# Background loads on GpSimd's queue, queries and keys made in steps, and the output projection's operand built during the last pairs

## The chip, the cores and the metric

The kernel runs on one core of one Trainium2 chip. The metric is device time in microseconds (us) of one execution; the median of three runs of the kernel before is 2591.47 us (2590.05 to 2592.86). Engines are named as in the profile: PE is TensorE, PEld its weight load, DVE VectorE, ACT ScalarE, POOL GpSimd, SP SyncE, which here only issues DMAs.

## The reference, cut to what matters

One encoder layer over 1024 tokens of width 2048, in float32:

```python
h = rms_norm(x, pre_g)
proj = jnp.einsum('btd,dn->btn', h, w_in)          # 2048 -> 11264 columns
q, k, v, z_a, u, vs, z_b, g_a, g_b = jnp.split(proj, SPLIT_POINTS, axis=-1)
y_a = neighbourhood_attention(q, k, v, rpb, rows)   # 8 heads, 8 x 16 window, softmax with a bias
y_a = y_a * jax.nn.silu(z_a)
y_b = spatial_gating(u, vs, ln_g, ln_b, w_s, b_s) * jax.nn.silu(z_b)   # u * (W_s LN(vs) + b)
merged = (jax.nn.sigmoid(g_a) * jnp.einsum('btc,cd->btd', y_a, w_pa)
          + jax.nn.sigmoid(g_b) * jnp.einsum('btc,cd->btd', y_b, w_pb))
out = jnp.einsum('btd,de->bte', merged, w_out)
return x + rms_norm(out, post_g)
```

## The kernel before, in words

Each float32 operand is split in two float32r parts, a high one that ACT copies and a low one that DVE subtracts (`split`, L118); a product is three matmuls, high x high, high x low, low x high. `product` (L149) issues twelve matmuls of 128x512 for a weight block of 512 rows by 128 columns: one *step* of the sequence `seq` (L807).

The input projection and the two branch projections are cut in *pairs* of 2 x 128 output columns and 1024 input rows. A `Pair` (L159) computes its 2x2 blocks by Winograd's form of Strassen's scheme with seven products (p1, p2, p6, p5, p7, p4, p3) instead of eight: DVE forms the sums of weight blocks s1 to s4 (`prepare`), the sums t1 to t4 of the left operand are made once per operand (`Left`, L248), and `evacuate` brings the banks A, B and C back by ACT copies and DVE additions. A `PlainPair` (L215) takes eight products. The 2048 input rows make two halves f of 44 pairs each; the results of the first are stored in DRAM blocks `d_dram`, those of the second are added there by accumulating stores. All these stores are DMAs on POOL's queue (`store`, L288). Then come eight pairs for w_pb and eight for w_pa, whose results, times their gates, are stored and accumulated in `m_dram`; then the output projection with w_out.

The left operand (x for the halves, y_dram for the branches) lies split in eight slots of `apool`, named a0 to a7 with two tiles each. When the operand changes, `prepare_x` or `prepare_y` loads the next one into `ypool`, one yield per step, and `build` (L874) splits its parts into slots that the pair before no longer needs (`release`, L864). `build` runs `hook` as often as it takes until the sources have arrived.

The main loop (L911) does for each step: events due at this step, evacuation of the step before, a build, `hook()`, the weights' preparation for this step, the twelve matmuls, and preparation two steps ahead. `hook` advances the first generator of `tasks` by one yield; through it the rest of the layer runs beside the second half of the projections, in this order: `norms`, `values`, `layer_norms`, `gating` for 8 groups (4 yields each), `attention` for 8 heads, `first_gates` (sigmoids of the merge gates ahead of their use).

`attention` (L590) per head takes eight query tiles i in 11 yields: scores on PE into bank s; one DVE operation that adds the bias tile `bt` and finds the maximum `mx` (L651); the exponential and the scaling on ACT; transposes; products with `vk` three yields later; the gate `za`. The loads stand in SP's queue, in program order with the weights' loads (L141): raw queries and keys `qk` (`block`, L463), `vk` (L623), `za` (L629), bias (L636). `queries` and `keys` scale and split a head's `qk` tiles in one yield each. DMAs of one queue are issued in order, and a DMA whose buffer or source isn't ready holds those behind it.

In `gating` (L531), z is multiplied by r_rows (the tokens' 1/rms), passed through Silu, and multiplied by r_rows again; u is multiplied by it, and the result yb (one buffer) by u.

After the last step all pools are closed; tiles of the merged operand are loaded from `m_dram` on ACT's queue and split one by one (`load_merged`, `split_merged`, L999 to L1006) ahead of the step that uses them, w_out comes in chunks of 256 KB (`load_chunk`, L955). `wide_step` (L985) issues the twelve matmuls of one chunk for four token tiles.

## Time and profile before

| | |
|---|---|
| median of three runs | 2591.47 us |
| the profiled execution | 2593.09 us |
| its span | 2591.3 us |
| mean granted clock | 0.987 |
| PE, DVE, ACT, POOL busy | 97%, 55%, 41%, 14% |
| moved by DMA | 410.10 MB, mean 158 GB/s |

Matmuls are pipelined, so a busy PE is not a PE at its peak: how many matmuls are issued in a stretch tells more than its busy share. An idle time stands before the instruction that ended it, with what released it. The granted clock of a stretch is 1.00 at full speed and 0.50 at half.

### The profile page before, as it was taken

The numbers are of one execution on the slowest core, as the hardware profiler recorded it, in microseconds if no ns is written. First come the engines' busy times: TensorE is split into PE (matmuls) and PEld (weight loads), VectorE is DVE, ScalarE is ACT, GpSimd is POOL, SyncE is SP. The second block draws the span as 40 slices with busy tenths as digits, with TensorE's granted clock in tenths as the row PEclk, the third lists the DMA queues.
The fourth block names the chain that finished last, engine by engine and source line by source line (L and its number), as shares of the span: only waits on it lengthen the run. The fifth ranks groups of instructions, "written<-read, shape, count | busy, mean of one in ns | idle before, by whom it ended". The sixth has DMA issues, their size and how long they took to land.

```text
span 2591.3 us, 32620 instructions
## 1 busy us (share of the span) xinstructions
PE 2507.8 (97%) x11363; PEld 2074.0 (80%) x11363; DVE 1423.2 (55%) x2270; ACT 1058.0 (41%) x1883; POOL 358.6 (14%) x532
## 2 busy tenths in 40 slices
PE   7999999999999999999999888999999999899998
PEld 5888888888888788887787777788888888788887
DVE  6444444444444744577655544466676787542434
ACT  6533333333333534432365555544443434342332
POOL 1111111111111112122111111133311111000000
PEclk9999999999999999999999999999999999999999
DMA  5633333333334468777765566589975676753645
GB/s 174 209 126 110 117 106 115 106 110 118 106 114 171 98 130 212 159 176 179 172 175 144 134 158 157 142 240 279 235 195 161 223 170 152 184 162 98 203 121 192
DMA packets 240069, 410.10 MB, mean 158 GB/s; under 512 B 25736, under 2 KB 85152, under 8 KB 239264
## 3 DMA queue, kind: packets, MB, share of 16 engines
q1 hardware_dynamic: 178432, 253.30, 32.4%
q0 software_dynamic: 55968, 141.07, 23.4%
q10 hardware_dynamic: 5504, 13.65, 1.6%
q8 instruction: 89, 1.46, 0.2%
q14 instruction: 76, 0.62, 0.1%
HBM read 264.78 MB, written 143.13 MB: 157 GB/s over the span
## 4 chain that ended last, share of the span: by engine, by line
PE 54%; issue 32%; POOL 7%; ACT 2%; DMA 2%; DVE 1%; SPq 0%; POOLq 0%; ACTq 0%; DVEq 0%
PE A L153 23%; PE C L153 11%; PE B L153 6%; PE t L989 3%; PE A L989 3%; POOL m L293 2%; PE s L989 2%; PE B L989 2%; PE C L989 2%; PE v L989 2%; DMA bt<-bias 1%; POOL d_ga L293 1%; POOL g_gb L767 1%; POOL d_qk L293 1%; POOL d_zu L293 1%
## 5 line engine op out<-in xcount | busy, mean ns | idle before, releaser
L153 PE MATMUL A<-a,wh 128*128 128x512 f32 x3328 | 1037.8, 393 | 15.3 <-ACT wh L120 11.7
L153 PEld LDWEIGHTS A<-a,wh 128*128 128x128 f32 x3328 | 623.3, 189 | 143.4 <-ACT wh L120 13.0
L121 DVE TENSOR_TENSOR wl<-x,wh 128x512 fp32r<-128x512 f32 x616 | 423.3, 688 | 498.3 <-ACT wh L120 495.3
L153 PE MATMUL A<-a,wl 128*128 128x512 f32 x1664 | 652.2, 392 | 7.3 <-DVE wl L121 7.0
L153 PE MATMUL C<-a,wh 128*128 128x512 f32 x1664 | 521.2, 395 | 7.0 <-ACT wh L120 4.5
L120 ACT CAST wh<-x 128x512 fp32r<-128x512 f32 x616 | 380.9, 619 | 280.5 <-PE C L153 220.9
L202 ACT COPY u<-A 128x512 f32<-128x512 f32 x300 | 176.3, 588 | 524.5 <-PE A L153 522.1
L153 PEld LDWEIGHTS A<-a,wl 128*128 128x128 f32 x1664 | 314.3, 189 | 77.2 <-DVE wl L121 10.7
L153 PEld LDWEIGHTS C<-a,wh 128*128 128x128 f32 x1664 | 313.7, 190 | 72.5 <-ACT wh L120 5.8
L153 PE MATMUL C<-a,wl 128*128 128x512 f32 x832 | 327.7, 394 | 1.7 <-DVE wl L121 1.6
L197 DVE TENSOR_TENSOR u<-C,u 128x512 f32<-128x512 f32 x200 | 138.0, 690 | 244.8 <-ACT u L202 154.5
L153 PE MATMUL B<-a,wh 128*128 128x512 f32 x864 | 269.9, 393 | 1.8 <-ACT a L410 0.9
L153 PEld LDWEIGHTS B<-a,wh 128*128 128x128 f32 x864 | 162.4, 189 | 35.9 <-ACT a L410 1.3
L153 PEld LDWEIGHTS C<-a,wl 128*128 128x128 f32 x832 | 158.1, 190 | 36.9 <-DVE wl L121 3.4
L121 DVE TENSOR_TENSOR wl<-wr,wh 128x512 fp32r<-128x512 f32 x120 | 82.8, 691 | 188.8 <-ACT wh L120 188.8
L153 PE MATMUL B<-a,wl 128*128 128x512 f32 x432 | 170.2, 394 | 2.0 <-DVE wl L121 1.8
L120 ACT CAST wh<-wr 128x512 fp32r<-128x512 f32 x120 | 74.6, 623 | 215.7 <-PE t L989 187.4
L174 DVE TENSOR_TENSOR x<-x,x 128x512 f32<-128x512 f32 x200 | 137.7, 688 | 3.5
L120 ACT CAST wh<-s 128x512 fp32r<-128x512 f32 x100 | 62.0, 620 | 102.4 <-PE B L153 100.3
L989 PE MATMUL A<-wh,x 128*128 128x512 f32 x240 | 94.1, 392 | 5.6 <-ACT wh L120 3.2
L153 PEld LDWEIGHTS B<-a,wl 128*128 128x128 f32 x432 | 81.8, 189 | 21.2 <-DVE wl L121 4.2
L292 ACT COPY c<-A 128x512 f32<-128x512 f32 x88 | 51.7, 587 | 111.1 <-PE A L153 111.1
(181 smaller groups left out, 2605.9 us busy)
## 6 DMA issues: line engine op xcount, KB each, us to landing
x<-w_units SPq DMA_DIRECT2D x288, 256.0 KB
wr<-w_out SPq DMA_DIRECT2D x120, 256.0 KB
d_zu<-u POOLq DMA_DIRECT2D x48, 256.0 KB, 3.9
d_qk<-u POOLq DMA_DIRECT2D x48, 256.0 KB, 3.9
d_gb<-u POOLq DMA_DIRECT2D x48, 256.0 KB, 3.6
d_ga<-u POOLq DMA_DIRECT2D x48, 256.0 KB, 4.1
m<-u POOLq DMA_DIRECT2D x48, 256.0 KB, 4.2
x<-w_v SPq DMA_DIRECT2D x32, 256.0 KB
```

The lines of the kernel that those rows point to most:

```text
L120: nc.scalar.copy(out=hi, in_=src)
L121: nc.vector.tensor_tensor(out=lo, in0=src, in1=hi.bitcast(F32), op=ALU.subtract)
L153: nc.tensor.matmul(acc, lhsT=wt[:, j * P:(j + 1) * P], rhs=operand[j // 2][:, j % 2, part], start=(first and j == 0 and n == 0), stop=(j = ...
L174: nc.vector.tensor_tensor(out=out, in0=in0, in1=in1, op=op)
L197: nc.vector.tensor_tensor(out=out, in0=in0, in1=out, op=ALU.add)
L202: nc.scalar.copy(out=u, in_=acc["A"])
L292: nc.scalar.copy(out=t, in_=bank)
L293: nc.gpsimd.dma_start(out=dst[c], in_=t, **({"accum_op": ALU.add} if accumulate else {}))
L767: nc.gpsimd.dma_start(out=g_dram[pr][c], in_=t)
L989: nc.tensor.matmul(acc[i], lhsT=stat[:, part, t * P:(t + 1) * P], rhs=wt, start=(kt == 0 and part == 0 and wt is chunk[0]), stop=(kt == nk ...
```

## The change

Five parts. (1) `block`, `fetch_values` and `fetch_gate` issue their loads on POOL's queue (`nc.gpsimd`) instead of SP's. Bias tiles have four buffers instead of three and are requested three tiles ahead instead of two. (2) A head's queries and keys are made in four steps (`prelude`: scale the queries, split them, scale the keys, split them), at yields 7 to 10 of the head before; the yield between two heads is gone. (3) In `gating`, Silu stands a yield behind the multiplication of z, u is multiplied by r_rows in place of the second multiplication of z, and yb has two buffers. (4) At the start x comes by SP's queue alone and the first two weight blocks by ACT's, and the sums of the first left operand take the scale by g with them (`scaled_less`), in another order. The pool for the second half's operand is opened three pairs ahead instead of two. (5) `merges` is a task: it loads merged tiles on POOL's queue, the first two into a pool of their own, the others into slots of `apool` as the last pair's products let go of them; the first four chunks of w_out are loaded six steps before the projections end, into the weights' buffers; `hook()` is called in the output projection too. The pools are placed anew for it.

```diff
-    for w, name in zip(NAMES, ("x11", "x21", "x12", "x22")):
+    first.load(("x11", "x21"), nc.scalar)
+    for w, names in zip(NAMES, ((), (), ("x12",), ("x22",))):
         for j in range(4):
-            load_x(first_x[j // 2][w][:, j % 2], 0, w, j, nc.gpsimd if j % 2 else nc.sync)
-        first.load((name,))
+            load_x(first_x[j // 2][w][:, j % 2], 0, w, j, nc.sync)
+        first.load(names)
...
+        def scaled_less(jj, w, other, dst):
+
+            s = left.src[jj]
+            for j in range(2):
+                kt = x_tile(0, w, 2 * jj + j)
+                nc.vector.scalar_tensor_tensor(out=s[dst][:, j], in0=s[w][:, j], scalar=g_cols[:, kt:kt + 1],
+                                               in1=s[other][:, j], op0=ALU.mult, op1=ALU.subtract)
...
+        for step in (((t1, 0),), ((t1, 1), (t2, 0)), ((t2, 1), ("t2", 0)), (("t2", 1), (t3, 0)), ((t3, 1), ("t1", 0)),
+                     (("t1", 1), (t4, 0)), (("t3", 0), (t4, 1)), (("t3", 1),), (("t4", 0),), (("t4", 1),)):
...
     def block(pool, pr, n, hf, tag, bufs):
 
         t = pool.tile([P, HALF], F32, tag, bufs=bufs)
-        nc.sync.dma_start(out=t, in_=d_dram[pr][2 * n + hf])
+        nc.gpsimd.dma_start(out=t, in_=d_dram[pr][2 * n + hf])
         return t
...
+        yield
+        for hf in range(2):
             nc.scalar.activation(z[hf], z[hf], AF.Silu)
-        yield
         if ("zu", g + 1) in complete:
             fetch_group(g + 1)
         for hf in range(2):
-            nc.vector.tensor_tensor(out=z[hf], in0=z[hf], in1=r_rows[:, hf * HALF:(hf + 1) * HALF], op=ALU.mult)
+            nc.vector.tensor_tensor(out=u[hf], in0=u[hf], in1=r_rows[:, hf * HALF:(hf + 1) * HALF], op=ALU.mult)
...
-            yb = bpool.tile([P, HALF], F32, "yb")
+            yb = bpool.tile([P, HALF], F32, "yb", bufs=2)
...
+        def prelude(h):
+
+            return [lambda: scaled(h, 0), lambda: queries(h), lambda: scaled(h, 1), lambda: keys(h)]
...
-                nc.sync.dma_start(out=vk[:4 * w, b], in_=v_dram[h, :, COL0[b]:COL0[b] + w])
+                nc.gpsimd.dma_start(out=vk[:4 * w, b], in_=v_dram[h, :, COL0[b]:COL0[b] + w])
...
-                nc.sync.dma_start(out=zs[:, hf * HALF:(hf + 1) * HALF], in_=d_dram[("za", h // 2)][2 * (h % 2) + hf])
+                nc.gpsimd.dma_start(out=zs[:, hf * HALF:(hf + 1) * HALF], in_=d_dram[("za", h // 2)][2 * (h % 2) + hf])
...
-            bts[(h, i)] = pool.tile([P, KROWS * 32], F32, "bt", bufs=3)
+            bts[(h, i)] = pool.tile([P, KROWS * 32], F32, "bt", bufs=4)
...
-                    if i < 6:
-                        fetch_bias(h, i + 2)
+                    if i < 5:
+                        fetch_bias(h, i + 3)
                     scores(h, i)
...
-                if i == 5 and ("head", h + 1) in complete:
+                if i == 3 and ("head", h + 1) in complete:
                     fetch(h + 1)
...
+                    following = prelude(h + 1)
+                if following and i >= 7:
+                    following[i - 7]()
+                    if i >= 8:
+                        fetch_bias(h + 1, i - 8)
+                yield
             nc.gpsimd.dma_start(out=y_dram[h], in_=zs)
             del kept[h]
-            yield
...
-        at(where[(n - 2, "p1")], open_ypool, prepare)
+        at(where[(n - (3 if n == K2 else 2), "p1")], open_ypool, prepare)
...
+    def merges():
+
+        nonlocal mpool0, mpool
+        mpool0 = Pool(tc, "mpool0")
+        mpool = Pool(tc, "mpool")
+        raw = {}
+        for d in range(NDT + 1):
+            if d < NDT:
+                while ("m", d // 2) not in complete:
+                    yield
+                raw[d] = mpool.tile([P, T], F32, "mr", bufs=2)
+                for hf in range(2):
+                    nc.gpsimd.dma_start(out=raw[d][:, hf * HALF:(hf + 1) * HALF], in_=m_dram[d // 2][2 * (d % 2) + hf])
+            yield
+            if d:
+                d -= 1
+                while d >= 2 and (d - 2) // 2 >= len(free):
+                    yield
+                places[d] = (mpool0, f"m{d}") if d < 2 else (apool, f"a{free[(d - 2) // 2]}_{d % 2}")
+                merged[d] = x8(d)
+                split(merged[d][:, 0], merged[d][:, 1], raw.pop(d))
+            yield
...
+        if k == len(seq) - 6:
+            loaded.extend(load_chunk(n) for n in range(LOADS))
+        if k == len(seq) - 1:
+            advance(0)
...
             for kt in range(NDT - (LATE if last else 0)):
-                if tg == 0 and ep == 0 and kt + 2 < NDT:
-                    split_merged(kt + 2)
-                    if kt + 4 < NDT:
-                        load_merged(kt + 4)
+                while kt not in merged or kt == NDT - 1 and mpool:
+                    hook()
                 for e in range(2):
                     wide_step([a[e] for a in acc], merged[kt], kt, tiles, next_chunk())
                     step_active()
+                    hook()
```

How this moves instructions, at three places. First SP's queue, from the second bias load of one head (the fourth) on, before; bt is a bias tile, vk, za and qk are the head's other loads, x the weights' blocks of the projections:

```order
L636 DMA bt<-bias 128x384
L623 DMA vk<-v_dram 96x1x512
L623 DMA vk<-v_dram 128x1x512 x2
L623 DMA vk<-v_dram 96x1x512
L636 DMA bt<-bias 128x384
L636 DMA bt<-bias 128x288
L141 DMA x_11947<-w_units 128x512
L141 DMA x_11949<-w_units 128x512
L636 DMA bt<-bias 128x288
L629 DMA za<-d_za_2_186 128x512
L629 DMA za<-d_za_3_187 128x512
L636 DMA bt<-bias 128x384
```

and a head's stretch of the same queue now:

```order
L672 DMA bt<-bias 128x384
L672 DMA bt<-bias 128x288
L141 DMA x_12063<-w_units 128x512
L141 DMA x_12146<-w_units 128x512
L672 DMA bt<-bias 128x288
L672 DMA bt<-bias 128x384
L141 DMA x_12258<-w_units 128x512
L141 DMA x_12260<-w_units 128x512
L672 DMA bt<-bias 128x384
L672 DMA bt<-bias 128x288
```

Bias and weights are left in SP's queue; the four vk, two za and four qk loads of a head are gone from it.

Second, POOL's queue in attention, from one head's store of y_dram on, before; d_qk and d_za are result blocks of the projections, stored from the tiles u and c:

```order
L731 DMA y_dram_69<-za 128x1024
L293 DMA d_qk_3_167<-u_11462 128x512
L293 DMA d_qk_2_166<-c_11539 128x512
L293 DMA d_za_0_188<-u_11499 128x512
L293 DMA d_qk_1_165<-u_11402 128x512
L293 DMA d_za_3_191<-u_11759 128x512
```

and now:

```order
L762 DMA y_dram_69<-za 128x1024
L659 DMA vk<-v_dram 96x1x512
L659 DMA vk<-v_dram 128x1x512 x2
L659 DMA vk<-v_dram 96x1x512
L293 DMA d_qk_3_167<-u_11458 128x512
L665 DMA za<-d_za_0_184 128x512
L665 DMA za<-d_za_1_185 128x512
L293 DMA d_qk_2_166<-c_11535 128x512
L492 DMA qk<-d_qk_0_160 128x512
L492 DMA qk<-d_qk_1_161 128x512
L492 DMA qk<-d_qk_2_162 128x512
L492 DMA qk<-d_qk_3_163 128x512
```

The stores keep their order, and ten loads of a head now stand between them, za behind the y_dram store that reads the same buffer.

Third, DVE in gating, from the last multiplication of one group to the first steps of the next, before; wl is the low part of a weight block, bs the bias of the spatial gating:

```order
L563 TENSOR_TENSOR yb<-yb,u 128x512
L121 TENSOR_TENSOR wl<-s_9436,wh 128x512
L197 TENSOR_TENSOR u_9403<-C,u_9403 128x512
L542 SCALAR_TENSOR_TENSOR bs<-t,lnb,bs 128x128
L545 TENSOR_TENSOR z<-z,r_rows 128x512 x2
L121 TENSOR_TENSOR wl<-x_9215,wh 128x512
L551 TENSOR_TENSOR z<-z,r_rows 128x512 x2
L121 TENSOR_TENSOR wl<-x_9428,wh 128x512
```

and now:

```order
L590 TENSOR_TENSOR yb<-yb,u 128x512
L121 TENSOR_TENSOR wl<-s_9430,wh 128x512
L197 TENSOR_TENSOR u_9397<-C,u_9397 128x512
L568 SCALAR_TENSOR_TENSOR bs<-t,lnb,bs 128x128
L571 TENSOR_TENSOR z<-z,r_rows 128x512 x2
L121 TENSOR_TENSOR wl<-x_9209,wh 128x512
L578 TENSOR_TENSOR u<-u,r_rows 128x512 x2
L121 TENSOR_TENSOR wl<-x_9422,wh 128x512
```

The place of the second multiplication of z is taken by that of u, whose load stands in POOL's queue behind the y_dram store of the group before.

## Rows read from the trace of the kernel before

**Rows 1.** The page's first part: engine, busy us, share, instructions.

```profile
PE 2507.8 (97%) x11363; PEld 2074.0 (80%) x11363; DVE 1423.2 (55%) x2270; ACT 1058.0 (41%) x1883; POOL 358.6 (14%) x532
```

**Rows 2.** The chain of waits, 150 to 200: start, us, what.

```profile
162.38 2.72 PE B L153 x12
```

**Rows 3.** Windows by stage: length, busy time (instructions) by engine, clock, DMA share, GB/s.

```profile
10.65:56.47 45.82, 38.99 (x144) 29.92 (x145) 36.76 (x46) 32.65 (x52) 2.71 (x5) 0.93 0.48 145
847.66:857.43 9.77, 7.55 (x25) 5.50 (x24) 5.71 (x7) 7.88 (x13) 1.08 (x2) 0.83 0.19 58
1125.99:1248.57 122.58, 114.94 (x553) 94.60 (x552) 93.36 (x153) 41.01 (x72) 24.63 (x34) 0.97 0.75 186
1281.31:1694.18 412.87, 373.51 (x1910) 314.59 (x1909) 215.41 (x470) 228.55 (x463) 50.81 (x62) 0.95 0.60 151
2209.26:2245.69 36.43, 29.47 (x110) 22.29 (x108) 17.17 (x23) 12.45 (x18) 3.49 (x5) 0.91 0.73 182
```

**Rows 4.** Windows of clean steps, one group of gating and parts of heads.

```profile
1128.86:1141.79 12.93, 12.93 (x69) 11.02 (x68) 9.41 (x16) 4.96 (x9) 2.29 (x3) 1.00 0.72 189
1485.76:1495.86 10.10, 10.10 (x49) 8.59 (x50) 7.40 (x17) 5.18 (x12) 3.15 (x4) 1.00 0.82 184
1295.38:1299.52 4.14, 4.14 (x25) 3.65 (x25) 2.62 (x6) 2.23 (x6) 0.00 (x0) 1.00 0.96 324
1346.72:1374.42 27.70, 27.70 (x158) 24.22 (x157) 15.90 (x37) 19.69 (x41) 2.55 (x3) 1.00 0.57 144
```

**Rows 5.** Waits of PE in attention: who for whom, us, times, longest.

```profile
PE s L647 <- DVE mx L651: 30.4, 7, 9.0
```

**Rows 6.** Waits of all engines in attention.

```profile
DVE pr L651 <- DMA bt<-bias: 51.6, 7, 12.2
```

**Rows 7.** Window of the last two microseconds of one stop.

```profile
1448.00:1450.00 2.00, 0.00 (x0) 0.00 (x0) 0.00 (x0) 0.00 (x0) 0.00 (x0) 0.50 0.54 194
```

**Rows 8.** Timeline of SP's queue before that stop: start, us, what.

```profile
1430.97 4.05 SPq L623 DMA_DIRECT2D vk<-v_dram  x4
1435.37 5.13 SPq L636 DMA_DIRECT2D bt<-bias  x2
```

**Rows 9.** Timeline of DVE at its end; in brackets the idle time before.

```profile
1450.45 0.56 DVE L651 CUSTOM_DVE_ANT_0 pr<-s,bt 128x384 f32<-128x384 f32 x1 [10.18 <-DMA bt<-bias]
```

**Rows 10.** The tile y_dram, 1100 to 1700: its stores (ns, min/median/max) and their landing.

```profile
L564 POOL DMA_DIRECT2D y_dram<-yb x16: 561/572/577, 1138.0 to 1253.1; - x16
...
DMA to landing us min/median/max: 2.3/4.2/8.7
```

**Rows 11.** Waits of all engines in gating.

```profile
DVE yb L560 <- DMA y_dram<-yb: 19.0, 8, 3.2
```

**Rows 12.** Timeline of DVE in gating, between two groups.

```profile
1171.93 0.69 DVE L563 TENSOR_TENSOR yb<-yb,u 128x512 f32<-128x512 f32 x1
...
1176.49 0.69 DVE L121 TENSOR_TENSOR wl<-x,wh 128x512 fp32r<-128x512 f32 x1 [1.21 <-ACT wh L120]
1177.10 1.29 DVE L551 TENSOR_TENSOR z<-z,r_rows 128x512 f32<-128x512 f32 x2
```

**Rows 13.** Timeline of POOL at the same place.

```profile
1174.12 0.85 POOL L293 DMA_DIRECT2D d_zu<-u  x1 [0.63 <-DVE bs L542]
```

**Rows 14.** The tile y, 0 to 60: landing of POOL's loads.

```profile
DMA to landing us min/median/max: 6.6/8.0/9.0
```

**Rows 15.** Timeline of ACT at the start.

```profile
4.25 0.72 ACT L410 ACTIVATE a<-y,g_cols 128x512 fp32r<-128x512 f32 x1 [1.57 <-DMA g_cols<-pre_g]
8.14 1.95 ACT L410 ACTIVATE a<-y,g_cols 128x512 fp32r<-128x512 f32 x3 [3.17 <-DMA y<-x_t]
9.99 0.60 ACT L120 CAST wh<-x 128x512 fp32r<-128x512 f32 x1
```

**Rows 16.** Groups of instructions: busy us, mean ns, idle before.

```profile
L121 DVE TENSOR_TENSOR x<-mr,x 128x1024 fp32r<-128x1024 f32 x16 | 19.6, 1226 | 9.5 <-ACT x L120 9.5
```

**Rows 17.** Window of the last steps of the projections.

```profile
2200.00:2210.00 10.00, 10.00 (x46) 8.29 (x45) 8.14 (x13) 3.81 (x8) 2.58 (x3) 1.00 0.63 137
```

More of the change, by code (lines that the diff above doesn't have):

```diff
@@ L687, in attention @@
         for h in range(H):
-            while h not in raw and h not in kept:
-                if ("head", h) in complete:
-                    fetch(h)
+            if h not in kept:
+                while ("head", h) not in complete:
                     yield
-                yield
-            if h not in kept:
-                queries(h)
-                yield
-            if len(kept[h]) < 2:
-                keys(h)
-                yield
-            if (h, 0) not in bts:
-                fetch_bias(h, 0)
-            fetch_bias(h, 1)
+                fetch(h)
+                for i in range(3):
+                    fetch_bias(h, i)
+                    yield
+                for f in prelude(h):
+                    f()
+                    yield
             fetch_values(h)
-            yield
+            following = None
             for i in range(11):
@@ L890, in build @@
             ypool.close()
+            if left is left_of[3]:
+                begin(merges)
     def need(left, part):
@@ L894, in need, with x8 @@
             build()
+    LATE = 4
+    LOADS, AHEAD = 4, 2
+    jobs, loaded, ready = [], [], []
+    taken = [0]
+    active = []
+    for tg in range(2):
+        for ep in range(2):
+            jobs += [w_out[kt, 2 * ep + e] for kt in range(NDT) for e in range(2)]
+    del jobs[-2 * LATE:]
+    mpool0 = mpool = None
+    merged, places = {}, {}
+    def x8(d):
+        pool, tag = places[d]
+        return pool.tile([P, 2, 2, HALF], F32R, tag).rearrange("p a b t -> p a (b t)")
+    def merges():
[8 more added lines that the diff above has]
+                raw[d] = mpool.tile([P, T], F32, "mr", bufs=2)
+                for hf in range(2):
+                    nc.gpsimd.dma_start(out=raw[d][:, hf * HALF:(hf + 1) * HALF], in_=m_dram[d // 2][2 * (d % 2) + hf])
[3 more added lines that the diff above has]
+                while d >= 2 and (d - 2) // 2 >= len(free):
+                    yield
+                places[d] = (mpool0, f"m{d}") if d < 2 else (apool, f"a{free[(d - 2) // 2]}_{d % 2}")
+                merged[d] = x8(d)
+                split(merged[d][:, 0], merged[d][:, 1], raw.pop(d))
+            yield
+        mpool.close()
+        mpool = None
@@ new lines, in load_chunk, with advance @@
+    def load_chunk(n):
+        raw = wpool.tile([P, HALF], F32, ("x11", "x12")[n % 2], bufs=2)
+        nc.sync.dma_start(out=raw, in_=jobs[n])
+        return raw
+    def advance(now):
+        while len(loaded) < min(now + LOADS, len(jobs)):
+            loaded.append(load_chunk(len(loaded)))
+            if len(ready) < len(loaded) - (LOADS - AHEAD):
+                ready.append(split_weights(loaded[len(ready)]))
+        while len(ready) < min(now + AHEAD, len(jobs)):
+            ready.append(split_weights(loaded[len(ready)]))
@@ new lines, in next_chunk, with step_active, wide_step @@
+    def next_chunk():
+        advance(taken[0] + 1)
+        pair = ready[taken[0]]
+        taken[0] += 1
+        return pair
+    def step_active():
+        for g in list(active):
+            if next(g, StopIteration) is StopIteration:
+                active.remove(g)
+    def wide_step(acc, stat, kt, tiles, chunk, nk=NDT):
+        for i, t in enumerate(tiles):
+            for part, wt in ((0, chunk[0]), (0, chunk[1]), (1, chunk[0])):
+                nc.tensor.matmul(acc[i], lhsT=stat[:, part, t * P:(t + 1) * P], rhs=wt,
+                                 start=(kt == 0 and part == 0 and wt is chunk[0]),
+                                 stop=(kt == nk - 1 and part == 1))
@@ L896, in hybrid_kernel, with wide_banks @@
+    def wide_banks(tiles):
+        return [[psum(a), psum(b)] for _, (a, b) in zip(tiles, (("A", "A"), ("B", "C"), ("s", "v"), ("t", "t")))]
     starting = first_builds()
@@ L980, in step_active @@
-    def step_active():
-        for g in list(active):
-            if next(g, StopIteration) is StopIteration:
-                active.remove(g)
-    def wide_step(acc, stat, kt, tiles, chunk, nk=NDT):
-        for i, t in enumerate(tiles):
-            for part, wt in ((0, chunk[0]), (0, chunk[1]), (1, chunk[0])):
-                nc.tensor.matmul(acc[i], lhsT=stat[:, part, t * P:(t + 1) * P], rhs=wt,
-                                 start=(kt == 0 and part == 0 and wt is chunk[0]),
-                                 stop=(kt == nk - 1 and part == 1))
@@ L993, in wide_banks @@
-    def wide_banks(tiles):
-        return [[psum(a), psum(b)] for _, (a, b) in zip(tiles, (("A", "A"), ("B", "C"), ("s", "v"), ("t", "t")))]
-    merged, raw_m = {}, {}
-    def load_merged(d):
-        raw_m[d] = p4.tile([P, T], F32, "mr", bufs=2)
-        for hf in range(2):
-            nc.scalar.dma_start(out=raw_m[d][:, hf * HALF:(hf + 1) * HALF], in_=m_dram[d // 2][2 * (d % 2) + hf])
-    def split_merged(d):
-        merged[d] = x8(d if d < 15 else 16)
-        split(merged[d][:, 0], merged[d][:, 1], raw_m.pop(d))
```

172 lines of the change are left out of this document (73 added, 99 removed).

## The prediction

> **What bounds the kernel.** I first read the busy shares [rows 1]: PE is busy 97% of the span, DVE 55%, ACT 41%, POOL 14%. That points at PE, but does not say how well it is fed, so the second view is the chain of waits in a clean stretch [rows 2]: twelve matmuls of 128x512, one step of the sequence, take 2.72 us. The program has 860 such steps (100 Pairs of 7 and 4 PlainPairs of 8 in the projections, 128 in the output projection), 2339 us of a span of 2591.3. The rest is small matmuls, which stay, and losses. For the losses I read busy time and clock by stage [rows 3] against clean steps [rows 4].
>
> - Start: the first matmul is at 10.65, and the 12 steps after it take 45.82 instead of 32.64: 13.2 lost.
> - Change of operand before the second half: two steps in 9.77, 4.3 lost.
> - Gating: 34 steps in 122.58. A clean group of four steps takes 12.93, 2.05 more than 4 x 2.72; 34 x 2.72 + 8 x 2.05 = 108.9, so 13.7 is lost.
> - Attention: 412.87 for 8 heads of 11 steps and 7 steps between heads. The clean pieces [rows 4] make one head: 10.10 (its first three steps) + 4.14 (the fourth) + 27.70 (the last seven) = 41.94. 8 x 41.94 + 7 x 2.72 = 354.6, so 58.3 is lost.
> - Way into the output projection: 9 steps in 36.43 instead of 24.48, 12.0 lost.
>
> That is 101.5, beside the 10.65 ahead of the first matmul. Over half is in attention. There PE stands still 412.87 - 373.51 = 39.4 us [rows 3], 30.4 of it in seven waits of the scores for DVE's mx [rows 5], and DVE is late because a bias tile is: 51.6 in seven waits [rows 6]. The other 18.9 of the 58.3 is mostly the half clock (1.2 instead of 2.4 GHz) behind a stop: the granted mean is 0.95 in this stage [rows 3] and was 0.50 late in one stop [rows 7]. So a microsecond of PE's wait costs 1.5 here. Why the bias is late stands in SP's queue [rows 8]: four vk loads are issued ahead of it, the issue of two bias loads then takes 5.13, and DVE waits 10.18 until the tile has landed [rows 9].
>
> **The change, part by part.**
>
> *Attention, loads.* vk, za and qk (10 DMAs a head) leave SP's queue for POOL's; bias goes from two steps ahead with 3 buffers to three with 4. SP then holds weights and bias alone. The mechanism that I take: bias waited for what stood ahead of it in one queue, not for the engines, since late in the stop, with PE, DVE, ACT and POOL all idle, the DMA share was only 0.54 [rows 7]. With one step more of lead (10.10 / 3 = 3.4 us) and four loads fewer ahead, all seven waits go: 30.4 x 1.5 = 45.6. *Attention, compute.* Scaling and splitting of queries and keys become four steps instead of two, so ACT's casts no longer stand behind a DVE operation of the same step. Of the 12.7 that is left of the loss I let 5 stay: 53 gained. Bounds: 58.3, and 0 if bias lands as late as now.
>
> The Trainium skill says in DMA: Bandwidth & Descriptors, section Issuing engines are not separate DMA queues, that the DMAs of all issuing engines run on the same 16 engines, and that issuing from several saves issue time alone; by it the move of vk is worth little, and the time would be that of rival A. The same page, section Queues, rings and completion order, has each engine take turns between queues, which would let bias pass vk. The 0.54 agrees better with the second; no run here has vk on another queue.
>
> *What POOL takes on.* Per head 10 issues of 0.57 (a plain issue, [rows 10]), 5.7 us in 42, on an engine that is 14% busy. The stores of u and c wait behind them. The za load waits for the landing of the y_dram store of the head before (one za buffer), up to 8.7 [rows 10]; it stands two steps behind that store now, four before. The u1 buffer is used again seven steps later, some 26 us in this stage, so I cost these waits at nothing; rivals B and C are the cases in which that cover is gone.
>
> *Gating.* Two of DVE's waits go: yb for its own store, 19.0 in eight [rows 11], by a second buffer, and a wl in each group, 1.21 [rows 12], whose cast stands behind the Silu that waits for z: 9.7 in eight. One comes: u is multiplied by r_rows a step before it was needed, and its loads go to POOL behind the y_dram store. From the end of the last yb multiply (1172.62) to the place where u stands now (1177.10) DVE has 4.5 less 1.2 of wait, 3.3 us of work [rows 12], and 3.9 to the second half. POOL needs 0.57 for the store, 0.57 for the first load, and in half of the groups 0.85 for a u store between [rows 13]. No row has a plain load on POOL here; the nearest are the y_dram stores, most of them of 256 KB, median 4.2 to landing [rows 10], and the loads at the start, median 8.0 with eight queued at once [rows 14]. I take 5, nearer to the stores, since POOL's queue is short here: 0.57 + 0.57 + 0.43 + 5 - 3.9 = 2.7 a group, 21.6 against the 28.7 removed. At 13.7 lost for 28.7 of DVE's waits 10.3 stays: 3.4 gained. Bounds: 13.7 gained (2.3 to landing, no wait), 8 lost (8.0 to landing, 5.7 a group).
>
> *Operand before the second half.* prepare_x needs 4 + 16 yields, one a step, but its pool opens 14 steps ahead, and build() then runs what is left at once, with ACT busy 7.88 of the 9.77 [rows 3]. It opens 21 steps ahead now: 4 of 4.3 gained, 0 if ACT is late for another reason.
>
> *Start.* x comes by SP alone, the first two weight blocks by ACT's queue, and 12 of 16 scalings on ACT become part of DVE's subtractions. Now ACT waits 3.17 for a tile by POOL's queue [rows 15], which took 6.6 or more to land [rows 14], while SP's first tile was there by 4.25. Four scalings 0.65 apart and the cast end at 4.25 + 2.6 + 0.6, say 7.7: 3 gained. Of the 13.2 behind it the wait for the weight block goes, and ACT's work shrinks by 12 x 0.65 = 7.8; DVE's stays. I take 7. Bounds for both: 0 and 16.
>
> *Output projection.* The merged tiles are loaded and split during the last steps and placed where the last pair's operands were; four weight chunks are loaded ahead. PE's idle time there, 36.43 - 29.47 = 7.0 [rows 3], and the half clock behind it go, 12.0 at most. But four splits of 1.23 [rows 16] now stand in DVE's last eight steps, and DVE was busy 8.14 of 10 there [rows 17]: 17.7 + 4.9 = 22.6 in 21.8. No slack is left, so I keep 3.5: 8.5 gained, and 0 if DVE falls behind.
>
> Sum: 53 + 3.4 + 4 + 10 + 8.5 = 78.9. The profiled execution took 2593.09 (the span of 2591.3 and 1.8 around it), which gives 2514.2; the median shown is 1.6 lower, so **2512.6**, with a range of its own from 2495 to 2526.
>
> **Rivals.**
>
> *A: the engines, not the queue, make bias late* (or the weight loads ahead of it, which wait for buffers, so that the move doesn't do what it says). For it: a DMA share of 0.60 over the stage and 0.73 to 0.75 in two others [rows 3]. Against: 0.54 in the stop. Then only the lead helps: 3.4 off each of seven waits of 4.3 on average and 9.0 at most [rows 5] leaves 7 to 13, say 10, x 1.5 = 15: 2527.
>
> *B: loads on POOL are slow, 8 to 9 us as at the start.* Gating loses 8 instead of gaining 3.4. And za is late for the fifth step of each head: 8.7 for the y_dram store and 8.5 for the load against 14.2 from the head's start (10.10 + 4.14) is 3 late, 8 x 3 x 1.5 = 36, and half of it if DVE's lead takes the rest. 2512.6 + 11.4 + 18 = 2542. For it: POOL serves one queue in order. Against: the stores on it land in 4.2.
>
> *C, slower: POOL's queue stands still.* A load that waits for a landing (qk for d_qk's accumulating store, za for y_dram's) holds the u stores behind it; ACT's next copy into u1 waits, every cast behind it too, and PE stops with the clock halved. It decides where POOL stands for longer than the 26 us of u1 less 9 for issue and landing, 17 us. To use up the gain it takes 78.9 / 8 = 9.9 a head, 6.6 of stop x 1.5; at 11 a head the time is 2512.6 + 88 = 2601. Against it: the longest landing of these on POOL is 9.0 [rows 14].
>
> *D: gains and new waits are equal*: 2586 to 2597.
>
> **Chances.** Forecast 0.64, A 0.15, B 0.13, C 0.06, D 0.02. The range from 2495 to 2548 holds the forecast, A and most of B; left out are C, D, a worse B, and a gain above 97. A measurement of this kernel tells a change of over 0.2%, 5.2 us, from none: faster 0.92, same 0.02, slower 0.06.
>
> **What would show it.** No wait of DVE for bt over 1 us, and heads of 42 to 43 us, show the main step; waits for bt in the same place, shorter by 3 to 4, show A. DVE's waits for u<-d_zu in gating tell what a load on POOL takes; waits for za or vk show B, ACT's waits for the landing of u show C. Steps of 2.72 through the start of the second half, and a first matmul before 8.5, show those parts; DVE without idle time and PE waiting for wl in the last eight steps of the projections show the price at the end. The prediction is wrong if a head still takes 52 us.

## The result and the profile after

The changed kernel takes 2527.8 us (median of four runs, 2526.07 to 2530.92), the kernel before 2590.76 beside it: ratio 0.9758, interval 0.9741 to 0.9775, 63 us faster. The forecast was 2512.6; the measured time lies in the range from 2495 to 2548, but 15 above the forecast and above the forecast's own range (up to 2526). The profiled execution is the quickest of the four (2526.07), its span 2524.2, 67.1 shorter than before's 2591.3.

The page's first part, which answers to [rows 1]:

```profile
PE 2485.5 (98%) x11363; PEld 2063.2 (82%) x11363; DVE 1421.7 (56%) x2284; ACT 1051.1 (42%) x1871; POOL 439.0 (17%) x669
```

The work is the same; POOL has 137 instructions more, nearly all of them loads. The same five stretches as in [rows 3] (columns as there), gating and attention with the two steps behind them, as in the table and in every run below:

```profile
9.21:45.13 35.92, 35.24 (x144) 28.31 (x145) 31.60 (x45) 24.78 (x39) 2.90 (x5) 1.00 0.58 180
839.36:844.80 5.44, 5.44 (x26) 4.50 (x24) 4.54 (x7) 3.55 (x6) 0.89 (x2) 1.00 0.32 100
1113.33:1240.32 126.99, 120.03 (x578) 97.55 (x576) 97.17 (x159) 42.74 (x75) 43.52 (x67) 0.99 0.74 189
1267.52:1643.24 375.72, 365.85 (x1934) 313.62 (x1933) 217.93 (x476) 231.81 (x468) 99.70 (x142) 0.99 0.73 173
2153.02:2178.47 25.45, 24.77 (x109) 20.19 (x108) 16.16 (x23) 11.52 (x17) 8.87 (x14) 1.00 0.93 252
```

The two longer ones in the kernel before:

```profile
1125.99:1254.11 128.12, 120.48 (x578) 99.20 (x576) 97.41 (x160) 42.14 (x75) 26.41 (x36) 0.97 0.75 184
1281.31:1699.71 418.40, 379.04 (x1933) 319.18 (x1933) 218.59 (x475) 229.70 (x465) 52.22 (x64) 0.96 0.60 152
```

| stretch | before | after | gained | forecast |
|---|---|---|---|---|
| first matmul at | 10.65 | 9.21 | 1.4 | 3 |
| the 12 steps behind it | 45.82 | 35.92 | 9.9, less 0.9 in the step behind | 7 |
| stop for the norms, loss in two steps | 2.4 | 4.5 | -2.1 | - |
| operand before the second half | 9.77 | 5.44 | 4.3 | 4 |
| gating and two steps behind it, 36 steps | 128.1 | 127.0 | 1.1 | 3.4 |
| attention and two steps behind it, 97 steps | 418.4 | 375.7 | 42.7 | 53 |
| into the output projection | 36.43 | 25.45 | 11.0 | 8.5 |

The rest differs by 0.2. A clean attention stretch of 97 steps is 41.94 x 8 + 9 x 2.72 = 360.0 by [rows 4].

What is left in attention is told by its waits (who for whom: us, times, longest):

```profile
POOL qk L492 <- DMA vk<-v_dram: 9.7, 8, 3.3
PE v L716 <- DMA vk<-v_dram: 6.3, 3, 2.7
DVE za L751 <- DMA za<-d_za: 6.1, 3, 3.5
```

DVE's waits for bt [rows 6] are gone. In their place PE itself waits for vk, and DVE for za; POOL stands ahead of its qk loads until vk has landed. One such stop on POOL, and PE behind it (start, us, what; idle time before in brackets):

```profile
1492.60 0.85 POOL L293 DMA_DIRECT2D d_qk<-u  x1 [2.56 <-DVE u L197]
1495.60 0.86 POOL L293 DMA_DIRECT2D d_za<-u  x1 [2.15 <-DVE u L197]
1496.13 0.88 POOL L762 DMA_DIRECT2D y_dram<-za  x1
1496.67 2.97 POOL L659 DMA_DIRECT2D vk<-v_dram  x4
1502.74 1.16 POOL L665 DMA_DIRECT2D za<-d_za  x2 [3.10 <-DMA y_dram<-za]
```
```profile
1507.00 0.91 PE L716 MATMUL v<-pk,vk 96*128 96x128 f32 x6 [2.66 <-DMA vk<-v_dram]
```

The last product of the head before ended at 1491.60, so the vk buffer was free; POOL issued the load 5.1 later, behind three stores, two of which waited for DVE to make their operand. The first of the four DMAs then took 10.2 to land, the last 12.7, and the DMA engines were full meanwhile. Over the eight heads:

```profile
DMA to landing us min/median/max: 7.2/10.2/12.7
```

The windows of two such stops:

```profile
1320.00:1333.00 13.00, 10.85 (x53) 9.10 (x52) 5.52 (x15) 6.04 (x14) 7.73 (x13) 0.93 1.04 221
1497.00:1511.00 14.00, 11.34 (x55) 9.32 (x54) 6.31 (x17) 7.06 (x16) 6.33 (x11) 0.91 1.06 237
```

Ahead of the last number of a window's row stand the clock and the DMA share: the share is 1.04 and 1.06 in these stops, the clock 0.93 and 0.91. In gating DVE waits for the loads of u, as the prediction had it, and behind that a matmul waits for DVE. The waits, and the longest of those for u on DVE's timeline:

```profile
DVE u L578 <- DMA u<-d_zu: 23.6, 9, 4.3
PE C L153 <- DVE u L197: 3.4, 2, 1.9
```
```profile
1153.48 1.44 DVE L578 TENSOR_TENSOR u<-u,r_rows 128x512 f32<-128x512 f32 x2 [4.34 <-DMA u<-d_zu]
```

The stop that nobody forecast stands at 146 us, where `norms` ends: PE transposes r_cols, which POOL computes. POOL comes to it behind a store:

```profile
145.81 0.54 POOL L293 DMA_DIRECT2D d_vs<-u  x1 [8.24 <-DVE r_cols L115]
146.37 2.21 POOL L116 TENSOR_TENSOR r_cols<-r_cols,neghalf 128x8 f32<-128x8 f32 x1
```
```profile
148.63 0.27 PE L473 MATMUL t<-ident,r_cols 128*8 128x128 f32 x1 [1.74 <-POOL r_cols L116]
```

The same wait was there before, 1.27 long. The tasks are at another place of the sequence now, and a lower clock behind the stop comes on top: from 135 to 160 the granted mean is 0.93, where it was 1.00 before.

### The profile page after: what moved, and what is told of

It is laid out like the page before. It is cut to its first block, busy times and chain, and to the rows that moved or that the text cites. A ratio compares the mean times of both kernels' runs of the same rounds, so it can differ in the third digit from the quotient of the medians.

```text
span 2524.2 us, 32543 instructions
## 1 busy us (share of the span) xinstructions
PE 2485.5 (98%) x11363; PEld 2063.2 (82%) x11363; DVE 1421.7 (56%) x2284; ACT 1051.1 (42%) x1871; POOL 439.0 (17%) x669
## 4 chain that ended last, share of the span: by engine, by line
PE 86%; issue 4%; DMA 4%; DVE 3%; ACT 2%; POOL 1%; POOLq 0%; SPq 0%; DVEq 0%; ACTq 0%
PE A L153 39%; PE C L153 20%; PE B L153 10%; PE t L1001 3%; PE A L1001 3%; PE v L1001 2%; PE s L1001 2%; PE C L1001 2%; PE B L1001 2%; DMA vk<-v_dram 1%; PE v L716 1%; DMA u<-d_zu 1%; DVE wl L121 1%; PE s L683 1%; PE t L516 1%
## 5 line engine op out<-in xcount | busy, mean ns | idle before, releaser
L153 PE MATMUL A<-a,wh 128*128 128x512 f32 x3328 | 1034.9, 392 | 10.4 <-ACT wh L120 9.2
L121 DVE TENSOR_TENSOR wl<-x,wh 128x512 fp32r<-128x512 f32 x736 | 505.8, 688 | 660.2 <-ACT wh L120 659.8
L120 ACT CAST wh<-x 128x512 fp32r<-128x512 f32 x736 | 455.9, 620 | 488.2 <-PE C L153 229.0
L292 ACT COPY c<-A 128x512 f32<-128x512 f32 x88 | 51.6, 586 | 127.0 <-PE A L153 127.0
L197 DVE TENSOR_TENSOR u<-B,u 128x512 f32<-128x512 f32 x100 | 68.8, 688 | 22.1 <-PE B L153 22.1
L1001 PE MATMUL A<-wh,a 128*128 128x512 f32 x208 | 80.9, 389 | 0.0
L1001 PE MATMUL t<-wh,a 128*128 128x512 f32 x208 | 80.9, 389 | 0.0
```

The costliest lines, as they stand in the source:

```text
L120: nc.scalar.copy(out=hi, in_=src)
L121: nc.vector.tensor_tensor(out=lo, in0=src, in1=hi.bitcast(F32), op=ALU.subtract)
L153: nc.tensor.matmul(acc, lhsT=wt[:, j * P:(j + 1) * P], rhs=operand[j // 2][:, j % 2, part], start=(first and j == 0 and n == 0), stop=(j = ...
L197: nc.vector.tensor_tensor(out=out, in0=in0, in1=out, op=ALU.add)
L292: nc.scalar.copy(out=t, in_=bank)
L1001: nc.tensor.matmul(acc[i], lhsT=stat[:, part, t * P:(t + 1) * P], rhs=wt, start=(kt == 0 and part == 0 and wt is chunk[0]), stop=(kt == nk ...
```

## The experiments

Theory Q is the prediction's: bias waited for the loads ahead of it in SP's queue. Against it stand L (the longer lead of bias is what gains), A (the DMA engines), and later the burst: the four vk loads, issued at once behind the last use of one buffer, make late whatever is needed next, on any queue. Run 5 calls it S and run 11 calls it B, which is not the prediction's rival B. Single profiles of the same attention code differed by 8 us (375.7 in the changed kernel, 383.9 in the run with u ahead below), so smaller differences are judged by the times. Ratios are to the kernel before, run beside each.

**1. Bias's lead alone, on the kernel before**

```diff
-            bts[(h, i)] = pool.tile([P, KROWS * 32], F32, "bt", bufs=3)
+            bts[(h, i)] = pool.tile([P, KROWS * 32], F32, "bt", bufs=4)
...
-                    if i < 6:
-                        fetch_bias(h, i + 2)
+                    if i < 5:
+                        fetch_bias(h, i + 3)
```

> The kernel before with one edit: bias tiles have four buffers and are requested three tiles ahead instead of two; all loads stay in SP's queue. Theory Q (SP's queue: bias waits for the loads issued ahead of it): the four vk loads still stand ahead of bias, one step of lead is 3.4 us, each of the seven stops gets shorter by up to 3.4, 10 us x 1.5 = 15, time 2576 (2570 to 2582), DVE's waits for bt some 30 us instead of 51.6. Theory L (the lead is what the change gains by, the queue adds nothing): most of the 45 goes, time near 2546, DVE's waits for bt under 10 us.

2568.76 us, ratio 0.9914 (0.9897 to 0.993). The attention stretch and DVE's waits:

```profile
1281.06:1678.47 397.41, 375.07 (x1934) 316.36 (x1933) 218.34 (x475) 230.06 (x465) 52.20 (x64) 0.97 0.63 160
```
```profile
DVE pr L651 <- DMA bt<-bias: 30.0, 6, 9.3
```

The waits are as Q had it (30.0), the gain is 21 instead of 15, a little beyond Q's range: between the two, nearer to Q.

**2. The loads on POOL's queue alone, on the kernel before**

```diff
-        nc.sync.dma_start(out=t, in_=d_dram[pr][2 * n + hf])
+        nc.gpsimd.dma_start(out=t, in_=d_dram[pr][2 * n + hf])
...
-                nc.sync.dma_start(out=vk[:4 * w, b], in_=v_dram[h, :, COL0[b]:COL0[b] + w])
+                nc.gpsimd.dma_start(out=vk[:4 * w, b], in_=v_dram[h, :, COL0[b]:COL0[b] + w])
...
-                nc.sync.dma_start(out=zs[:, hf * HALF:(hf + 1) * HALF], in_=d_dram[("za", h // 2)][2 * (h % 2) + hf])
+                nc.gpsimd.dma_start(out=zs[:, hf * HALF:(hf + 1) * HALF], in_=d_dram[("za", h // 2)][2 * (h % 2) + hf])
```

> The kernel before with one edit: vk, za, qk and the gating blocks are loaded by POOL's queue; bias keeps three buffers and two tiles of lead, and there is still one more step between two heads. Theory Q: all seven waits of DVE for bt go, time 2545 (2540 to 2556), vk is in time because its load is issued four steps ahead of its use. Theory L: bias is late as before, time 2585 to 2591. Rival A (the 16 DMA engines): bias waits move or stay, DMA share near 1.0 in the stops, time 2580 or more.

2569.4 us, ratio 0.9921 (0.9903 to 0.9939). Gating, then attention; and the waits:

```profile
1127.48:1263.02 135.54, 123.63 (x577) 101.47 (x576) 98.75 (x161) 42.04 (x75) 43.47 (x67) 0.95 0.73 179
1290.22:1680.57 390.35, 372.46 (x1933) 312.36 (x1933) 218.72 (x475) 229.97 (x465) 99.97 (x140) 0.99 0.69 163
```
```profile
DVE za L719 <- DMA za<-d_za: 11.4, 4, 3.4
PE v L680 <- DMA vk<-v_dram: 3.9, 3, 2.4
DVE pr L651 <- DMA bt<-bias: 3.1, 1, 3.1
```

Bias is nearly cured, as Q says, and attention gains 28.1. The weights' loads are still in SP's queue here, so they alone were not what held bias. But za and vk are late now, and gating pays 7.4. The whole is worth 21, not 45, a time that none of the three theories had.

**3. Both**

The edits of 1 and 2 together.

> The kernel before with both edits: loads by POOL's queue and bias three tiles ahead with four buffers; queries and keys are still made in two steps and there is still the step between two heads. Theory Q: as with the loads moved alone, within 5 us (2540 to 2556), so the lead is worth little once the queue is free. Theory L: 10 us or more faster than with the loads moved alone. What is left over 355 us in attention is then the work of two steps (queries, keys), which the change spreads over four.

2566.32 us, ratio 0.9903 (0.9888 to 0.9919): within 5 us of each alone, as Q had it, so they don't add up; the time is above Q's range (2540 to 2556), as in run 2.

```profile
1284.48:1673.29 388.81, 370.29 (x1934) 311.07 (x1933) 218.53 (x475) 229.97 (x465) 99.98 (x140) 1.00 0.69 163
```

The step from here to the changed kernel's attention (375.7) is 13.1: queries and keys in four steps, and no step between heads.

**4. The changed kernel with vk back on SP's queue**

```diff
-                nc.gpsimd.dma_start(out=vk[:4 * w, b], in_=v_dram[h, :, COL0[b]:COL0[b] + w])
+                nc.sync.dma_start(out=vk[:4 * w, b], in_=v_dram[h, :, COL0[b]:COL0[b] + w])
```

> The changed kernel with vk's four loads back on SP's queue, all else as changed. In the changed kernel PE waits 6.3 us for vk in three places (some 10 us with the half clock behind them). Theory P (POOL's queue makes vk late, because stores that wait for their operands stand ahead of it and it is issued 4 to 5 us after the last use of the buffer): on SP vk is in time, but bias stands behind it again; PE's waits for vk go (-10) and waits of DVE for bt come back, each shorter by the lead; net 2520 to 2545. Theory E (the DMA engines are full while vk, za and qk come together, share 0.98 to 1.06 there): vk lands as late as now, 9 to 12 us after its issue, PE still waits for it, and bias is late as well; 2530 to 2560.

2542.98 us, ratio 0.9817 (0.98 to 0.9834), 15 slower than the changed kernel.

```profile
DVE pr L687 <- DMA bt<-bias: 46.4, 7, 9.9
PE s L683 <- DVE mx L687: 19.8, 7, 6.1
```

PE waits for vk no longer, and bias is late again: theory P, at the upper end of its range. Theory E's range holds the time too, but it wanted PE to wait for vk still. The waits for bias are hardly shorter than the 51.6 of [rows 6], where P had taken the lead off each. SP issues vk when the buffer comes free (at 1503.29 in one head, where the last product ended at 1503.26), POOL up to 5 us later.

**5. vk in four tiles, loaded block by block**

```diff
-            vk = pool.tile([P, 4, 4, P], F32, "vk")
-            for b in range(4):
-                w = KW[b]
-                nc.gpsimd.dma_start(out=vk[:4 * w, b], in_=v_dram[h, :, COL0[b]:COL0[b] + w])
+            vks[(h, b)] = pool.tile([P, 4, P], F32, f"vk{b}")
+            nc.gpsimd.dma_start(out=vks[(h, b)][:4 * w], in_=v_dram[h, :, COL0[b]:COL0[b] + w])
...
                     weighted(h, i - 3)
+                    if i >= 7 and h + 1 < H:
+                        fetch_values(h + 1, i - 7)
```

> The changed kernel with vk in four tiles, one per block of columns, each loaded for the next head as soon as its last product in this head is issued (yields 7 to 10), by POOL's queue; same bytes, same buffers in all. In the changed kernel the loads of vk, za and qk come within some 10 us of a head's start, and PE waits for vk in three heads (6.3 us, some 10 with the half clock). Theory S (the burst behind the last use of one large buffer makes vk late): waits of PE for vk go, heads of 42 to 43.5 us, 2517 (2512 to 2521). Theory P2 (POOL's queue makes loads late wherever they stand, since stores that wait are ahead of them): vk is still late in some heads, or za and qk in its place; within 4 us of 2527.8.

2515.22 us, ratio 0.9708 (0.9694 to 0.9723), 12.6 faster than the changed kernel: theory S.

```profile
1270.57:1632.28 361.71, 361.17 (x1934) 311.72 (x1932) 218.17 (x476) 231.94 (x468) 100.73 (x142) 1.00 0.74 180
```

Attention is 1.7 above the clean 360.0. Waits for vk, za and bt are all gone, with the same bytes, queue and buffers.

**6. The same, and za in two halves**

```diff
-            zs = pool.tile([P, T], F32, "za")
+            zs = pool.tile([P, HALF], F32, f"za{hf}")
...
+                if i in (5, 6):
+                    nc.scalar.activation(kept[h][i - 3], kept[h][i - 3], AF.Silu)
+                if i == 6:
+                    store_y(h, 0)
```

> As the run before, and za in two tiles of half the columns: the first half is loaded at yield 0 and stored to y_dram at yield 6, so that its load no longer waits for the store at the head's end. DVE waited for za in three heads of the changed kernel (6.1 us). Theory S: those waits go as well, all heads 42 to 42.5 us, 2513 (2509 to 2518). Theory P2: no gain over the run before.

2535.23 us, ratio 0.9786 (0.9771 to 0.98): 20 slower than the run before, which neither theory had. Silu in two yields makes ACT load its function tables again; the groups of ACT in attention, in run 5 and then here (busy us, mean ns, idle before):

```profile
L690 ACT ACT_TABLE_LOAD x9 | 11.5, 1283 | 0.2
L757 ACT ACT_TABLE_LOAD x8 | 10.3, 1283 | 0.1
```
```profile
L692 ACT ACT_TABLE_LOAD x17 | 21.8, 1283 | 0.3
L759 ACT ACT_TABLE_LOAD x16 | 20.5, 1283 | 0.3
```

Sixteen loads more, 20.5 us of ACT. (The Trainium skill, ScalarE: Activation LUTs, section What ACT_TABLE_LOAD costs, has 1283 ns for a load, as here, and a drain of some 1380 ns with it, which this trace doesn't show: all 33 loads together have 0.6 of idle time ahead of them, and the ACTIVATE behind the load at 1344.97 starts 0.02 after its end.) PE waits for what ACT makes:

```profile
PE t L706 <- ACT pr L698: 8.4, 11, 1.4
PE v L718 <- ACT pk L708: 5.2, 6, 1.5
```

**7. u a group ahead, on the changed kernel**

```diff
+        u = [block(bpool, ("zu", g), 1, hf, "u", 4) for hf in range(2)]
-        fetched[g] = z, wst, bs
+        fetched[g] = z, u, wst, bs
...
-            yb = bpool.tile([P, HALF], F32, "yb", bufs=2)
+            yb = z[hf]
```

> The changed kernel with one edit in gating: u of the next group is loaded with z of the next group, a group ahead (four u tiles; yb is written into z's tile, which is free then, so that it fits). In the changed kernel DVE waits 23.6 us for u in nine waits, longest 4.3, and gating keeps 12 of loss. Theory U (the wait for u is what keeps gating's loss): DVE's waits for u go and 8 to 12 are gained, 2518 (2515 to 2521). Rival (DVE and ACT have no slack there, or z's load now waits for y_dram's store in z's tile): 0 to 3 gained.

2511.56 us (2506.32 to 2519.88), ratio 0.9697 (0.9675 to 0.9719): theory U, with 16 gained at the median where 8 to 12 were expected.

```profile
1112.28:1226.63 114.35, 114.35 (x578) 97.20 (x577) 99.28 (x161) 42.64 (x75) 43.17 (x67) 1.00 0.85 213
```

Gating's stretch has no stop left: 12.6 less than in the changed kernel, and DVE's waits for u are gone.

**8. Runs 6 and 7 together, and one more step ahead of the norms' transposes**

```diff
         rsqrt_into(r_cols, r_cols, 1.0 / D, RMS_EPS)
         yield
+        yield
```

> The changed kernel with all of these, and one more step between the norms' last operation on POOL and the transposes that read it (the stop at 146 us, 4.5 lost). Sum of the terms if each holds: vk 10, za 4, u 10, norms 4: 2527.8 - 28 = 2500 (2496 to 2508). If the burst only moves elsewhere, 2512 or more.

2519.06 us, ratio 0.9723 (0.9707 to 0.9739). The za halves of run 6 spoil it (attention 383.9; gating 114.3). The norms' loss was 2.5 here, 4.5 in the changed kernel and 2.9 in run 7, which has no such edit: what the step is worth stays open. PE no longer waits for r_cols there, but 1.37 for the load of by_group that its next transpose reads.

**9. Runs 5 and 7 together**

> The changed kernel with two edits together: vk in four tiles that are loaded as their blocks come free (alone 2515.2), and u a group ahead with yb in z's tile (alone 2511.6). In their profiled runs attention's stretch of 97 steps was 361.7 with the first and gating's stretch of 36 steps 114.4 with the second, against 375.7 and 127.0 in the changed kernel. If the two don't touch each other: 2527.8 - 14.0 - 12.6 = 2501 (2497 to 2505). If the time that one frees is taken by the other's waits, 2508 or more.

2500.24 us (five runs, 2499.03 to 2501.49), ratio 0.9645 (0.9632 to 0.9658): they add up. It beats the kernel before by 3.6%, and the changed one by 27.6 us.

```profile
1114.12:1228.46 114.34, 114.34 (x577) 97.20 (x576) 99.50 (x161) 42.62 (x75) 43.27 (x67) 1.00 0.85 212
1255.66:1617.36 361.70, 361.16 (x1934) 311.67 (x1932) 218.20 (x476) 231.84 (x468) 100.79 (x142) 1.00 0.74 180
```

**10. The changed kernel with all loads back on SP's queue**

The three lines of experiment 2, the other way.

> The changed kernel with all loads of vk, za, qk and of the gating blocks back on SP's queue, all else as changed (bias three ahead, queries and keys in four steps). It tells what the four steps bring without POOL's queue. In the kernel before with the lead alone, attention's stretch was 397.4; with lead and POOL's queue 388.8, and 375.7 when the four steps come to it. Theory Q: bias stands behind vk again and is late, so attention is near 390, as with vk alone on SP, and gating about as before, 2543 (2536 to 2552). If the four steps by themselves do most of it, attention is under 380 and the time under 2532.

2519.24 us, ratio 0.9719 (0.9706 to 0.9732): 8.6 faster than the changed kernel. Neither theory had this: without the part of the change that the prediction held for the main one, the kernel is faster.

```profile
1112.89:1227.24 114.35, 114.35 (x577) 97.20 (x576) 98.53 (x161) 42.62 (x75) 26.38 (x36) 1.00 0.83 210
1254.44:1637.56 383.12, 368.73 (x1933) 316.14 (x1932) 216.96 (x476) 230.67 (x468) 52.87 (x66) 0.98 0.68 170
```
```profile
DVE pr L687 <- DMA bt<-bias: 30.1, 5, 7.4
PE s L683 <- DVE mx L687: 11.3, 4, 3.5
```

Gating loses nothing with its loads on SP. In attention bias is late again, yet PE waits only 11.3 for DVE. One of these bias loads was issued from 1529.40 on, behind vk's four, and landed 16.3 later, and on the way the DMA engines were full, in the second of these windows:

```profile
1530.00:1536.00 6.00, 6.00 (x31) 5.13 (x30) 3.76 (x10) 3.65 (x9) 1.46 (x2) 1.00 0.77 202
1536.00:1542.00 6.00, 6.00 (x36) 5.23 (x35) 1.41 (x3) 1.99 (x5) 1.11 (x2) 1.00 1.06 268
1542.00:1548.00 6.00, 2.46 (x13) 2.10 (x12) 0.98 (x3) 1.69 (x5) 0.00 (x0) 0.77 0.59 179
```

The third window is the stop, at a share of 0.59, as 0.54 was in [rows 7]: when PE stands still, the burst is nearly over.

Runs 7 and 10 have the same gating time, 114.35, and differ in attention by the queue: 2511.56 against 2519.24, with intervals that overlap a little (0.9675 to 0.9719, 0.9706 to 0.9732). With the burst left in, POOL's queue is most likely worth some 8 in attention, and it costs 12.6 in gating.

Run 4 differs from this one, in attention, by za and qk alone, which it loads on POOL's queue. SP's queue then holds fewer loads, and yet DVE waits longer for bias: 46.4 against 30.1 here, one profile each.

**11. All loads on SP, and vk block by block**

The edits of 10 and 5 together, the vk loads on SP too.

> The changed kernel with all loads back on SP's queue (alone 2519.2) and vk in four tiles that are loaded as their blocks come free, a block a step from yield 7 to 10; attention's stretch was 383.1 with the loads on SP, 375.7 with all on POOL, 361.7 with all on POOL and vk block by block. Theory B (the burst: vk, issued all at once behind the last use of one buffer, fills the engines and makes late whatever is needed next, bias on SP's queue, vk itself on POOL's): no waits of DVE for bt over 1 us, attention 361 to 366, time 2500 (2497 to 2504); the queue is then worth nothing. Theory Q (a queue that bias shares with the other loads makes it late): bias still late in some heads, attention 374 or more, 2511 or more.

2499.16 us, ratio 0.9643 (0.9628 to 0.9657): theory B, the burst, and the best time with run 9. One wait for bias is over 1 us, where it wanted none:

```profile
1255.38:1617.01 361.63, 361.08 (x1934) 311.69 (x1932) 217.95 (x476) 232.03 (x468) 52.88 (x66) 1.00 0.72 180
```
```profile
DVE pr L687 <- DMA bt<-bias: 2.7, 2, 2.5
```

vk stands in one queue with bias, in turn with it, and bias is in time but for these 2.7. 361.63 on SP, 361.71 and 361.70 on POOL: with vk block by block the queue makes no difference.

**12. Four steps alone: run 10 with bias as before**

Run 10 with the edit of 1 the other way (three buffers, two tiles ahead).

> The changed kernel with all loads on SP's queue and bias as before (three buffers, two tiles ahead): of the changes in attention only the four steps for queries and keys are left. It gives the fourth corner: attention's stretch was 418.4 before, 397.4 with the lead, 383.1 with lead and four steps. If lead and steps add up: 418.4 - 14.3 = 404, and 2519.2 + 21 = 2540 (2535 to 2546). If the steps alone remove most of it (bias late only because the engines' work of two crowded steps held it): under 390, under 2527.

2556.16 us, ratio 0.986 (0.9844 to 0.9877).

```profile
1255.00:1672.89 417.89, 377.12 (x1933) 322.89 (x1932) 217.81 (x476) 231.76 (x468) 52.90 (x66) 0.95 0.63 157
```
```profile
DVE pr L687 <- DMA bt<-bias: 62.4, 8, 11.0
```

Neither guess: in attention the four steps alone gain nothing (417.9 against 418.4), though with the lead they gain 14.3 (397.4 to 383.1). DVE's waits for bias have grown from 51.6 [rows 6] to 62.4: without the longer lead, the time that the four steps save is spent waiting for bias.

## Why the prediction was right or wrong

The direction and the stage that pays held, and 67.1 of the 78.9 came, by the spans; the mechanism of the largest term did not hold. That the time lies between 2495 and 2548 is owed to the room left there for rivals A and B, since the forecast's own range ends at 2526. By its steps:

- *Start*: the sum is right (10.4 after forecast 10), its split isn't. The first matmul came at 9.21, not before 8.5: ACT's fourth scaling waited for x until 7.93, and the cast stands behind it. The twelve steps gained more than 7.
- *Operand before the second half*: right, 4.3 of 4.3; its steps take 2.72 each.
- *Output projection*: right in kind, too cautious. DVE's extra splits found room: the last steps have no wait for wl, and the first steps of the output projection take 2.72 each.
- *Gating*: the net is near (1.1 against 3.4), and the wait is what was forecast: 23.6 in all against 21.6, 4.3 at the longest against 2.7 on average. A load of u on POOL landed in 5.6 (median in gating) where 5 was taken. What the other edits gain was right: on SP's queue 13.8 of loss go (run 10, 128.1 to 114.35), where 13.7 was put. What the wait for u costs was too small: 12.6 (run 7), where 10.3 was put.
- *Attention, loads*: the step that failed. It had "all seven waits go: 30.4 x 1.5 = 45.6", with the new waits on POOL's queue costed at nothing. The seven went, but the move of the loads gained 28.1 alone (run 2) and 29.6 with the lead (run 3), since vk and za became late themselves. Over the whole kernel the move loses: with all loads left on SP's queue the time is 8.6 shorter (run 10). Of the two signs of the main step one came, no wait for bt; a head takes 43.9 on average (375.7 less nine steps of 2.72, by eight), not 42 to 43. Rival B had priced za and not vk; its longer landings came true for vk (7.2 to 12.7), and part of its loss with them.
- *Attention, compute*: 7.4 of 12.7 was forecast, 13.1 came with the loads on POOL (388.8 to 375.7), 14.3 on SP, nothing without bias's lead (run 12). It is no term of its own.
- *Not forecast*: the norms' stop, 2.1.

The misses by the table are -10.3 in attention, -2.3 in gating, -2.1 in the norms, -0.2 in the rest, and +0.4, +0.3 and +2.5 in the other three: -11.7, against 67.1 - 78.9 = -11.8 by the spans.

The time is that of rival A (2527), and the trace isn't: A wanted waits for bt in the same place, and there is none. A's mechanism may still have had a part in it. The prediction set the engines aside because of a share of 0.54 late in one stop [rows 7]. Just ahead of that stop, in the kernel before, the share was 0.90, and in the changed kernel's stops it is over 1:

```profile
1440.00:1444.00 4.00, 3.62 (x21) 2.94 (x19) 0.28 (x2) 0.61 (x1) 0.00 (x0) 1.00 0.90 231
1444.00:1448.00 4.00, 0.00 (x0) 0.00 (x0) 0.00 (x0) 0.00 (x0) 0.00 (x0) 0.92 0.53 157
```

So the 0.54 alone did not rule the engines out. Nor does the 0.90 prove them: for the last 6 of the 10.18 that DVE waits [rows 9] the share was 0.53 and 0.54, and the tile was still on its way. Two comparisons tell more. Between the changed kernel and run 4 only vk's queue differs: with vk on POOL's, DVE doesn't wait for bias, with vk on SP's it waits 46.4. So it counts whether vk stands ahead of bias in its own queue. Between run 4 and run 10 only the queue of za and qk differs in attention: DVE waits 46.4 with them on POOL's and 30.1 on SP's. So it seems to count, too, what another queue loads meanwhile.

So the cause is told better by the burst (theory S of run 5): a head's four vk loads came at once, because one buffer was free only after the last product. On SP's queue they made bias late, on POOL's queue vk and za. Spread over the last four steps of the head before, they make next to nothing late on either queue (runs 5 and 11). Run 5 issues them earlier and also apart; which of the two does it was not told apart, nor how much of bias's wait, in the kernel before, was its place in the queue and how much the full engines.

The Trainium skill says in DMA: Bandwidth & Descriptors, section Issuing engines are not separate DMA queues, that issuing from several engines saves only issue time, since all end on the same 16 engines. The prediction gave the rule too little weight: with vk block by block 2499.16 on SP and 2500.24 on POOL agree with it (gating's stretches are equal there, 114.35 and 114.34). With the burst left in, the queue did matter, by what it made late: bias on SP's, vk and za on POOL's.

## What to carry to other kernels

Before loads are moved to another queue, ask what lets them be issued only so late: a buffer that is released whole, by its last use, turns its reload into a burst, and splitting it by use (run 5) costs a few lines. A share of the DMA engines is to be read from the start of a delay, not from its end, and a stop that PE shows is the end of it. And where one late operand sets the pace, the gains of other edits don't add up: the four steps are worth nothing without bias's longer lead (run 12) and 13 to 14 us with it.

## What the runs showed of the hardware that was not expected

- Silu in two yields instead of one brought ACT's table loads in attention from 17 to 33, 1283 ns each; the run with it is 20 us slower (run 6 against run 5), and 13.6 of PE's waits there are for ACT.
- A bias load of 128x288 took 16.3 us to land in a burst (from 1529.40 on in run 10, 3.4 of it its issue), against a median of 5.0 in the changed kernel's attention.
- The move of gating's loads cost nearly as much as its other edits had gained (12.6 of 13.8), through waits of at most 4.3 at a time.
- With fewer loads in SP's queue, and za and qk on POOL's, bias behind vk was later and not earlier (46.4 of waits in run 4, 30.1 in run 10, one profile each).
